# The FFN down projection by seven half-size products in four chunks of the contraction

## The chip, the cores and the metric

The kernel runs on one core of a Trainium2 chip. The metric is the device time of one execution in microseconds (us); lower is better.

## The reference

One decoder layer on 512 tokens with a model width of 2048. Only the last part matters here:

```python
x = x + gt_a * y                                   # called x1 below
h = rms_norm(x, g_ffn[l]) * (1.0 + sc_f) + sh_f    # h2 below
x = x + gt_f * conv_ffn(h, w_up[l], w_conv[l], b_conv[l], w_down[l])

def conv_ffn(h, w_up, w_conv, b_conv, w_down):
    u = h @ w_up                                   # 2048 -> 2 * 5632
    ...                                            # causal convolution, width 3, per channel
    gate, val = jnp.split(conv, 2, axis=-1)
    return (jax.nn.silu(gate) * val) @ w_down      # 5632 -> 2048
```

The product silu(gate) * val is called f. All data are float32. The gate gt_f is a vector over the 2048 output channels.

## The kernel before, in words

**Precision.** Every large matrix product is made of three TensorE products of float32r operands: each operand is split into a high half (a ScalarE copy into float32r) and a low half (a VectorE subtraction), and high x high, high x low and low x high are added up in PSUM. `split` (L112) does this for activations and, in `seven`, for weights; `wtile` (L95) loads and splits weights elsewhere.

**Buffers.** `get` and `put` hand out 81 slots of 128 x 512 floats from a first-in, first-out list. There are five raw weight buffers (`rawq`) and three pairs of split weight buffers (`hi_b`, `lo_b`). PSUM has eight banks of 128 x 512. SyncE (SP) issues the weight loads, GpSimd (POOL) issues the loads and stores of scratch tensors in DRAM. Each engine, and each issuing queue, goes through its instructions in order; the program's scheduler sets that order when the kernel is built, so it need not be the order of the code.

**The seven products.** `seven` (L912) multiplies a two-by-two block matrix of weights by a two-by-two block matrix of activations with seven block products in place of eight. For an output pair of two 128-channel tiles, the activations (split into halves of the contraction and halves of the 512 tokens) and four sums of them are prepared once: r11, r21, r22, t1 to t4. The weight blocks come per pair from DRAM (four loads), and VectorE makes four combinations of them. Each of the seven products is 8 contraction tiles x 3 matmuls of 256 columns, and one evacuation (`e1` to `e7`) of 128 x 256 takes it, or a sum in PSUM, out. Steps are prepared two ahead of their matmuls. The last gate columns (`w_gs`) and 40 of the 44 column pairs of the up projection (`w_ups`) are computed in this way.

**The end of the layer.** `ev_o` (L1238) makes x1 with tokens on the partitions and stores it to `x1_d` by 16 POOL transfers. `x1_T` (L1256) transposes it, and h2 is computed from it in place (L1292 to L1294). `up_group(0)` computes the first four f tiles in the ordinary way, `seven` the other 40; `ffn_out` applies the convolution and the gate and stores each f tile (channels on partitions) to `f_d` on POOL. Then the 44 tiles are loaded back into slots (L1377), four rows of the gate gt_f are loaded (`gate_row`), and the down projection runs twice over the 44 contraction tiles, once for each half of the output channels. Each step there loads 128 x 1024 weights, splits them, splits the f tile, and issues 8 banks x 3 matmuls of 512 columns, with tokens on the output partitions. Per bank the end is one multiplication with the gate row (L1406), one addition of x1 (L1407), and the store to the output (L1408).

**Gate columns.** `ada_stream` and `flush_cols` compute the modulation vectors during the mixer. Blocks named in `gtr_d` are written to DRAM as rows; the others go to columns of `mod` by two VectorE operations.

Of the kernel before, what the change touches and what calls it, by code (L numbers as in the profile page):

```python
# [31 lines left out]
def trunk_layer_kernel(  # L32
# [3 lines left out]
    g_mkv_lat, w_mkv_up, g_qm, g_km, w_pa, w_pb, w_o, w_up, w_ups, w_conv, b_conv, w_down,  # L36
# [13 lines left out]
    PEU=((2, 5, 8, 11, 14),) * 2 + ((),) * 6,  # L50
):
# [698 lines left out]
    gtr_d = {cb: dram.tile([P, T], F32, name=f"gtr{cb}") for cb in (8, 9, 10, 11, 20, 21, 22, 23)}  # L750
# [161 lines left out]
    def seven(src, n_pairs, rs, pairs_of_banks, fin, tick=None, near_end=None):  # L912
        r11, r21, r22, t1, t2, t3, t4 = rs

        def load(j, blk):
            t = rawq.popleft()
            SP.dma_start(t[:, :WN], src[j, blk])
            return t

        def hilo(t):  # L920
            i = cnt["wt"] % NH
            cnt["wt"] += 1
            hi, lo = hi_b[i][:, :WN], lo_b[i][:, :WN]
            split(hi, lo, t[:, :WN])
            return hi, lo

        def comb(o, a, b, op):
            V.tensor_tensor(o[:, :WN], a[:, :WN], b[:, :WN], op)  # L928

        def pair_steps(j):  # L930
            bx, by = pairs_of_banks[j % len(pairs_of_banks)]
            X, Y, Z = bx[:, :HT], by[:, :HT], by[:, HT:]
            L, E = {}, {}

            def p1():
                L[11] = load(j, 0)
                L[21] = load(j, 1)
                return hilo(L[11])

            def p7():  # L940
# [4 lines left out]
                L[22] = load(j, 3)  # L945
                return r

            def p6():
# [3 lines left out]
                L[12] = load(j, 2)  # L952
# [22 lines left out]
            def e1():  # L975
                E["s"] = get()
                A.activation(E["s"][:, :HT], X, AF.Copy)

            def e7():
                A.activation(E["s"][:, HT:], Y, AF.Copy)  # L980

            def e6():
                E["s6"] = get()
                A.activation(E["s6"][:, :HT], X, AF.Copy)

            def e2():
                E["u1"] = get()
                V.tensor_tensor(E["u1"][:, :HT], Z, E["s"][:, :HT], ALU.add)  # L988

            def e5():  # L990
                E["u2"] = get()
                V.tensor_tensor(E["u2"][:, HT:], X, E["s"][:, HT:], ALU.add)
                put(E["s"])

            def e4():
                V.tensor_tensor(E["u2"][:, :HT], Y, E["s6"][:, :HT], ALU.add)
# [9 lines left out]
        steps = [st for j in range(n_pairs) for st in pair_steps(j)]  # L1006
# [451 lines left out]
```

## Time and profile before

| what | value |
|---|---|
| median of 3 runs (lowest, highest) | 2702.99 us (2700.71, 2704.31) |
| the profiled execution's own time | 2702.67 us |
| its span, first to last instruction | 2700.9 us |
| TensorE, VectorE, ScalarE, GpSimd busy | 98%, 72%, 43%, 9% of the span |
| mean granted TensorE clock | 0.993 |
| DRAM traffic | 390.56 MB read, 44.04 MB written |

Durations in the profile come from one execution. PE is TensorE, PEld its weight loads, DVE VectorE, ACT ScalarE, POOL GpSimd, SP SyncE. A row of the groups reads: line, engine, operation, output<-inputs, shapes, count, then busy us and mean ns of one, then the engine's idle time just before these instructions and what ended it. In a row of the stretches, each engine's busy us in the stretch stands with its instruction count. In the waits a row reads: who waited, for whom, us in total, times, longest.

### The profile page before, as it was taken

What the parts mean: (1) busy time and instruction counts of PE and PEld (TensorE: products, weight loads), DVE (VectorE), ACT (ScalarE), POOL (GpSimd) and SP (SyncE); (2) the same over time, 40 slices, a digit from 0 to 9 for tenths busy, and PEclk for the clock granted to TensorE, in tenths of its full rate; (3) what the DMA queues carried; (4) which work ended last, traced back from release to release, by engine and by line L of the source; (5) the groups of instructions that cost most, each with busy time, mean ns of one, the idle gap of its engine ahead of it and who ended that gap; (6) DMA issues with size and microseconds to landing.
All of it is one profiled execution on the core that took longest, in us unless ns stands there. A gap on an engine that the chain in (4) does not pass through costs nothing.

```text
span 2700.9 us, 40414 instructions
## 1 busy us (share of the span) xinstructions
PE 2648.9 (98%) x15616; PEld 2298.6 (85%) x15616; DVE 1942.6 (72%) x3059; ACT 1154.9 (43%) x1711; POOL 237.1 (9%) x459
## 2 busy tenths in 40 slices
PE   6999999998999999999999999999999999999999
PEld 5777687778997767788789999999999998888887
DVE  7977976688878667983778888888888873325323
ACT  4333434334444555322545555555555553223221
POOL 1001011110022223110000000000000040000000
PEclk8999899999999999999999999999999999999999
DMA  9943136664585478973223333333333383233232
GB/s 340 343 158 98 33 112 207 202 214 159 182 273 165 147 257 277 334 275 133 91 95 121 117 126 118 118 122 114 125 122 118 122 308 118 97 121 126 97 116 75
DMA packets 198389, 437.26 MB, mean 162 GB/s; under 512 B 20106, under 2 KB 61476, under 8 KB 198196
## 3 DMA queue, kind: packets, MB, share of 16 engines
q1 hardware_dynamic: 166516, 348.60, 38.2%
q0 software_dynamic: 31648, 86.08, 9.5%
q8 instruction: 122, 2.00, 0.3%
q14 instruction: 71, 0.58, 0.1%
q10 hardware_dynamic: 32, 0.01, 0.0%
HBM read 390.56 MB, written 44.04 MB: 161 GB/s over the span
## 4 chain that ended last, share of the span: by engine, by line
PE 79%; issue 13%; DMA 4%; DVE 3%; POOL 1%; ACT 0%; SPq 0%; POOLq 0%; DVEq 0%; ACTq 0%
PE bank L117 15%; PE bank L118 14%; PE bank L119 14%; PE bank L1020 10%; PE bank L1021 10%; PE bank L1022 10%; DMA slot<-in_w_ada 2%; PE bank L1156 1%; DMA gate<-slot 1%; PE bank L683 1%; DVE slot L547 0%; DMA slot<-in_x 0%; DMA raw<-in_w_ada 0%; PE bank L1157 0%; PE bank L1154 0%
## 5 line engine op out<-in xcount | busy, mean ns | idle before, releaser
L1020 PE MATMUL bank<-slot,whi 128*128 128x256 f32 x2688 | 754.8, 282 | 9.8 <-DVE slot L988 4.6
L1021 PE MATMUL bank<-slot,whi 128*128 128x256 f32 x2688 | 754.6, 281 | 0.2 <-DVE slot L114 0.2
L1022 PE MATMUL bank<-slot,wlo 128*128 128x256 f32 x2688 | 749.1, 281 | 1.6 <-DVE wlo L114 1.6
L105 ACT ACTIVATE whi<-raw 128x1024 fp32r<-128x1024 f32 (+4 forms) x270 | 280.8, 1041 | 727.1 <-PE bank L119 525.2
L118 PE MATMUL bank<-wlo,slot 128*128 128x512 f32 (+2 forms) x1472 | 574.6, 391 | 0.9 <-DVE wlo L106 0.9
L117 PE MATMUL bank<-whi,slot 128*128 128x512 f32 (+2 forms) x1472 | 566.5, 392 | 6.5 <-ACT slot L384 4.9
L119 PE MATMUL bank<-whi,slot 128*128 128x512 f32 (+2 forms) x1472 | 569.7, 390 | 0.0
L113 ACT ACTIVATE whi<-raw 128x1024 fp32r<-128x1024 f32 x336 | 356.6, 1061 | 442.5 <-PE bank L1021 339.5
L106 DVE TENSOR_TENSOR wlo<-raw,whi 128x1024 fp32r<-128x1024 f32 (+4 forms) x270 | 323.4, 1198 | 276.9 <-ACT whi L105 274.9
L1020 PEld LDWEIGHTS bank<-slot,whi 128*128 128x128 f32 x2688 | 507.8, 189 | 12.6 <-DVE slot L988 5.4
L1021 PEld LDWEIGHTS bank<-slot,whi 128*128 128x128 f32 x2688 | 506.5, 188 | 0.6 <-DVE slot L114 0.5
L1022 PEld LDWEIGHTS bank<-slot,wlo 128*128 128x128 f32 x2688 | 504.0, 189 | 1.9 <-DVE wlo L114 1.8
L114 DVE TENSOR_TENSOR wlo<-raw,whi 128x1024 fp32r<-128x1024 f32 x336 | 409.7, 1220 | 84.2 <-ACT whi L113 83.5
L117 PEld LDWEIGHTS bank<-whi,slot 128*128 128x128 f32 x1472 | 278.2, 189 | 69.1 <-ACT slot L384 5.0
L118 PEld LDWEIGHTS bank<-wlo,slot 128*128 128x128 f32 x1472 | 278.4, 189 | 61.8 <-DVE wlo L106 1.4
L119 PEld LDWEIGHTS bank<-whi,slot 128*128 128x128 f32 x1472 | 276.8, 188 | 60.4 <-issue 0.5
L118 PE MATMUL bank<-slot,whi 128*128 128x512 f32 (+1 forms) x656 | 262.8, 401 | 1.3 <-DVE slot L686 1.3
L117 PE MATMUL bank<-slot,whi 128*128 128x512 f32 (+1 forms) x656 | 259.2, 403 | 1.7 <-ACT slot L1293 1.0
L928 DVE TENSOR_TENSOR raw<-raw,raw 128x1024 f32<-128x1024 f32 x192 | 234.6, 1222 | 31.9 <-DMA raw<-in_w_ups 24.5
L119 PE MATMUL bank<-slot,wlo 128*128 128x512 f32 (+1 forms) x656 | 256.8, 401 | 0.5 <-DVE wlo L106 0.5
L114 DVE TENSOR_TENSOR slot<-slot,slot 128x512 fp32r<-128x512 f32 x152 | 102.4, 687 | 181.7 <-PE bank L118 175.2
L722 DVE SCALAR_TENSOR_TENSOR slot<-slot,c_act,slot 128x512 f32<-128x512 f32 x203 | 150.0, 747 | 32.6 <-DMA slot<-in_w_ada 30.9
(288 smaller groups left out, 2518.8 us busy)
## 6 DMA issues: line engine op xcount, KB each, us to landing
slot<-in_w_ada SPq DMA_DIRECT2D x344, 256.0 KB, 5.6
raw<-in_w_ups SPq DMA_DIRECT2D x160, 512.0 KB, 3.2
raw<-in_w_down SPq DMA_DIRECT2D x88, 512.0 KB, 3.6
raw<-in_w_in SPq DMA_DIRECT2D x50, 512.0 KB, 3.4
raw<-in_w_gs SPq DMA_DIRECT2D x32, 512.0 KB, 3.3
raw<-in_w_o SPq DMA_DIRECT2D x32, 512.0 KB, 6.2
f<-slot POOLq DMA_DIRECT2D x44, 256.0 KB, 2.4
slot<-f POOLq DMA_DIRECT2D x44, 256.0 KB, 7.0
```

Source lines behind the costliest of these rows:

```text
L105: A.activation(hi, raw[:, :w], AF.Copy)
L106: V.tensor_tensor(lo, raw[:, :w], r32(hi), ALU.subtract)
L113: A.activation(dst_hi, src, AF.Copy)
L114: V.tensor_tensor(dst_lo, src, r32(dst_hi), ALU.subtract)
L117: PE.matmul(o, lh, rh, start=first, stop=False)
L118: PE.matmul(o, lh, rl, start=False, stop=False)
L119: PE.matmul(o, ll, rh, start=False, stop=last)
L722: V.scalar_tensor_tensor(acc, ts[i], c_act[:, k:k + 1], acc, op0=ALU.mult, op1=ALU.add)
L928: V.tensor_tensor(o[:, :WN], a[:, :WN], b[:, :WN], op)
L1020: PE.matmul(o, wh[:, ks], rh, start=first and k == 0, stop=False, skip_group_check=True)
L1021: PE.matmul(o, wh[:, ks], rl, start=False, stop=False, skip_group_check=True)
L1022: PE.matmul(o, wl[:, ks], rh, start=False, stop=last, skip_group_check=True)
```

## The change

The down projection is moved into `seven`. The 44 f tiles are taken in 22 couples (an even and an odd tile: the two halves of the contraction), and the couples are cut into four chunks of 6, 6, 5 and 5 (`DH`). In each chunk the 2048 output channels are done as eight pairs, with channels on the output partitions and tokens along the columns; a product has 6 or 5 contraction tiles, and weight blocks are 768 or 640 columns wide.

- `f_out` stores no f tile any more. It writes quarters of it, or adds them by accumulating DMAs, into seven DRAM tensors per couple: the operands r11, r21, r22 and the sums t1 to t4. Negated copies come from ScalarE.
- `ahead` loads these operand sets on SP and splits them, from the last five up pairs on for chunk 0, and from the middle of each chunk for the next one, as slots allow.
- The results of chunks 0 to 2, times the gate (now a column, a per-partition factor of the evacuation), are added to x1 in DRAM by accumulating DMAs. In chunk 3 the accumulated x1 is loaded and added during the evacuation, which is then VectorE's in all seven products, and the result goes to the output.
- x1 is stored transposed, from `x1_T` in place of `ev_o`. The gate blocks 20 to 23 become columns of `mod`. The output is written as channels x tokens and turned on the host, which is outside the device time; the weights of the down projection are laid out in blocks beforehand.

```diff
-    gtr_d = {cb: dram.tile([P, T], F32, name=f"gtr{cb}") for cb in (8, 9, 10, 11, 20, 21, 22, 23)}
+    gtr_d = {cb: dram.tile([P, T], F32, name=f"gtr{cb}") for cb in (8, 9, 10, 11)}
...
+    def seven(work, pairs_of_banks, hook=None):
+        def pair_steps(n, p):
+            bx, by = pairs_of_banks[n % len(pairs_of_banks)]
             X, Y, Z = bx[:, :HT], by[:, :HT], by[:, HT:]
             L, E = {}, {}
+            W = p.K * P
+            g1, g2 = p.scale or (None, None)
...
+            def copy(o, b, g, x):
+                if x is not None:
+                    V.scalar_tensor_tensor(o, b, g, x, op0=ALU.mult, op1=ALU.add)
+                elif g is not None:
+                    A.activation(o, b, AF.Copy, scale=g)
+                else:
+                    A.activation(o, b, AF.Copy)
+            def plus(o, b, g, x):
+                if g is not None:
+                    V.scalar_tensor_tensor(o, b, g, x, op0=ALU.mult, op1=ALU.add)
+                else:
+                    V.tensor_tensor(o, b, x, ALU.add)
...
-                A.activation(E["s"][:, :HT], X, AF.Copy)
+                copy(E["s"][:, :HT], X, g1, E["x10"])
...
-                V.tensor_tensor(E["u2"][:, HT:], X, E["s"][:, HT:], ALU.add)
+                plus(E["u2"][:, HT:], X, g2, E["s"][:, HT:])
...
-                A.activation(E["u1"][:, HT:], X, AF.Copy)
-                fin(j, E["u1"], E["u2"])
+                copy(E["u1"][:, HT:], X, g1, E["x11"])
+                if p.plus:
+                    put(*E["x"])
+                p.fin(E["u1"], E["u2"])
...
-            G.dma_start(x1_d[db][tb], xs[tb])
...
             A.activation(t, bk[m], AF.Copy)
+            G.dma_start(x1_d[db * 4 + m], t)
             x1T.append(t)
...
-    f_d = [dram.tile([P, T], F32, name=f"f{j}") for j in range(NF_)]
+    KINDS = ("r11", "t3", "t2", "r21", "t1", "t4", "r22")
+    f_d = {n: [dram.tile([P, HT], F32, name=f"f{n}_{i}") for i in range(NF_ // 2)] for n in KINDS}
+    def f_out(j, t):
+        i = j // 2
+        q1, q2 = t[:, :HT], t[:, HT:]
+        neg = get()
+        n1, n2 = neg[:, :HT], neg[:, HT:]
+        def add(n, v):
+            G.dma_start(f_d[n][i], v, accum_op=ALU.add)
+        if j % 2 == 0:
+            A.activation(neg, t, AF.Copy, scale=-1.0)
+            G.dma_start(f_d["t1"][i], q2)
+            G.dma_start(f_d["t4"][i], q2)
+            G.dma_start(f_d["t2"][i], q1)
+            G.dma_start(f_d["t3"][i], q2)
+            G.dma_start(f_d["r11"][i], q1)
+            add("t1", n1)
+            add("t4", n1)
+            add("t2", n2)
+        else:
+            A.activation(n2, q2, AF.Copy, scale=-1.0)
+            G.dma_start(f_d["r21"][i], q1)
+            G.dma_start(f_d["r22"][i], q2)
+            add("t4", q1)
+            add("t2", q2)
+            add("t3", n2)
+            add("t4", n2)
+        put(t, neg)
...
-    seven(w_ups, NF_ - 4, operands(h2, tsum), [(bank[2 * i], bank[2 * i + 1]) for i in range(4)], ffn_out)
-    for t in h2 + [x for ts in tsum for x in ts]:
-        put(*t)
-    fr = []
...
-            G.dma_start(xt, x1_d[db][tb])
-            V.tensor_tensor(o, bank[i], gf[db], ALU.mult)
-            V.tensor_tensor(o, o, xt, ALU.add)
-            SP.dma_start(out[tb * P:(tb + 1) * P, db * 512:(db + 1) * 512], o)
...
+    def load_set():
+        c, n = todo.popleft()
+        ts = []
+        for i in range(DH[c]):
+            if i % 2 == 0:
+                ts.append(get())
+            SP.dma_start(ts[-1][:, (i % 2) * HT:(i % 2 + 1) * HT], f_d[n][base[c] + i])
+        coming.append((c, n, ts))
+    def split_set():
+        c, n, ts = coming.popleft()
+        for i, t in enumerate(ts):
+            hi, lo = getr(), getr()
+            w = min(T, (DH[c] - 2 * i) * HT)
+            split(hi[:, :w], lo[:, :w], t[:, :w])
+            put(t)
+            held_by[c][n] += [hi, lo]
+            ops[c][n] += [(hi[:, o:o + HT], lo[:, o:o + HT]) for o in range(0, w, HT)]
+    def need(c):
+        return (DH[c] + 1) // 2
+    def ahead(left):
+        c = todo[0][0] if todo else coming[0][0] if coming else None
+        if c is None or left > 35 or left > 8 and left % 2:
+            return
+        if coming and len(free) >= 2 * need(coming[0][0]) + SPARE:
+            split_set()
+        if todo and todo[0][0] <= c and len(coming) < 2 and len(free) >= need(todo[0][0]) + SPARE:
+            load_set()
+    SPARE = 8
+    def up_hook(q, n):
+        last = q - (n - 7)
+        if last == 0:
+            for t in h2[:KH]:
+                put(*t)
+        elif last in (1, 2, 4, 5):
+            for t in tsum[{1: 2, 2: 1, 4: 0, 5: 3}[last]]:
+                put(*t)
+        elif last == 6:
+            for t in h2[KH:]:
+                put(*t)
+        ahead(n - q)
+    all_banks = [(bank[2 * i], bank[2 * i + 1]) for i in range(4)]
+    rs = operands(h2, tsum)
+    work = [Pair(rs, lambda blk, i=i: w_ups[i, blk], ffn_out(i)) for i in range(NF_ - 4)]
+    n_up = len(work) * 7
+    def down_pair(c, j):
+        def fin(u1, u2):
+            for i, u in enumerate((u1, u2)):
+                n = 2 * j + i
+                if c < len(DH) - 1:
+                    G.dma_start(x1_d[n], u, accum_op=ALU.add)
+                else:
+                    SP.dma_start(out[n * P:(n + 1) * P, :], u)
+            put(u1, u2)
+        def plus():
+            ts = [get(), get()]
+            for i in range(2):
+                G.dma_start(ts[i], x1_d[2 * j + i])
+            return ts
+        o = ops[c]
+        return Pair(tuple(o[n] for n in ("r11", "r21", "r22", "t1", "t2", "t3", "t4")),
+                    lambda blk: w_downs[c][j, blk], fin, K=DH[c],
+                    scale=(mod[:, 80 + 2 * j:81 + 2 * j], mod[:, 81 + 2 * j:82 + 2 * j]),
+                    plus=plus if c == len(DH) - 1 else None)
+    work += [down_pair(c, j) for c in range(len(DH)) for j in range(KD // 2)]
+    def hook(q, n):
+        if q < n_up:
+            up_hook(q, n_up)
+            return
+        c, r = divmod(q - n_up, 56)
+        if r >= 49:
+            put(*held_by[c][KINDS[r - 49]])
+        ahead(0 if (coming or todo or [(0,)])[0][0] == c else 56 - r)
+    seven(work, all_banks, hook)
```

More of the change, by code (lines that the diff above doesn't have):

```diff
@@ L910, in sum_tiles, with __init__ @@
             put(raw[n])
[L912 to L931, printed above, removed]
+    class Pair:
+        def __init__(self, rs, load, fin, K=KH, scale=None, plus=None):
+            self.rs, self.load, self.fin, self.K, self.scale, self.plus = rs, load, fin, K, scale, plus
```

153 lines of the change are left out of this document (82 added, 71 removed).

## The prediction

> **What bounds the kernel now.** I read the page first, then the busy time by stretches, the groups by line and shape, the waits, and the timelines of the seams.
>
> ```profile
> span 2700.9 us, 40414 instructions
> PE 2648.9 (98%) x15616; PEld 2298.6 (85%) x15616; DVE 1942.6 (72%) x3059; ACT 1154.9 (43%) x1711; POOL 237.1 (9%) x459
> DVE  7977976688878667983778888888888873325323
> PEclk8999899999999999999999999999999999999999
> ```
> TensorE carries the span at an undisturbed clock; VectorE is high in the up projection (slices 21 to 32) and low in the down projection (the last eight). The stretches say it in numbers (busy us of PE, PEld, DVE, ACT, POOL, then clock, DMA share, GB/s):
>
> ```profile
> 1440.00:1640.00 200.00, 200.00 (x1691) 200.00 (x1690) 174.54 (x191) 108.59 (x141) 5.40 (x10) 1.00 0.34 120
> 2160.00:2200.00 40.00, 40.00 (x340) 40.00 (x339) 35.48 (x42) 25.29 (x36) 14.92 (x28) 1.00 0.71 251
> 2300.00:2400.00 100.00, 100.00 (x432) 80.77 (x431) 29.67 (x29) 24.40 (x30) 3.76 (x7) 1.00 0.33 113
> ```
> So both stages are bound by how many columns TensorE must stream. The change takes columns away from the down stage and gives VectorE work there: the question is whether VectorE still keeps up. The seams of the stage, from the PE timeline and the chain that ended last:
>
> ```profile
> 2202.20 0.28 PE L1022 MATMUL bank<-slot,wlo 128*128 128x256 f32 x1
> 2204.08 0.50 PE L117 MATMUL bank<-whi,slot 128*128 128x512 f32 x1 [1.60 <-ACT slot L113]
> 2694.20 0.47 issue
> 2696.58 0.69 DVE slot L1407
> ```
> Up ends at 2202.5, down runs 2204.1 to 2694.2 (490.1 us), and two VectorE operations and the last store end the span at 2700.9.
>
> **TensorE's part.** Before, down issues 2 halves x 44 tiles x 8 banks x 3 = 2112 matmuls of 512 columns: 490.1 / 2112 = 232.06 ns each. After, it issues 8 pairs x 7 products x 22 tile positions (6+6+5+5) x 3 = 3696 of 256 columns. Their price stands in the up stage, which runs the same seven products:
>
> ```profile
> L977 ACT ACTIVATE slot<-bank x40: 362/367/371, 1409.8 to 2186.3; 128x256 f32<-128x256 f32 x40
> ```
> This is the first evacuation of each pair: 39 pairs in 776.5 us, 19.91 us each, 168 matmuls of 118.54 ns. So 3696 x 118.54 = 438.1 us, **52.0 us less**. The two prices (232.06 and 118.54) give 5.0 ns fixed per matmul; the 1584 more matmuls cost 8 us of it, inside the term.
>
> The Trainium skill, "TensorE: Matmul & The Clock Gate", section "Back-to-back issue gap", speaks against this: sustained spacing 81 ns at 128 columns and 131 at 512, so halving the columns saves far less than half. A straight line between its figures puts 256 columns at 0.75 of 512, and the term would be an estimated 640 us. The trace disagrees: 118.54 against 232.06 is 0.51.
>
> **VectorE's part.** A pair splits seven weight blocks and makes four combinations, each K x 128 columns wide, now 768 or 640 instead of 1024, and the products are taken out with the gate as a factor.
>
> ```profile
> L114 DVE TENSOR_TENSOR wlo<-raw,whi 128x1024 fp32r<-128x1024 f32 x336 | 409.7, 1220 | 84.2 <-ACT whi L113 83.5
> L114 DVE TENSOR_TENSOR slot<-slot,slot 128x512 fp32r<-128x512 f32 x152 | 102.4, 687 | 181.7 <-PE bank L118 175.2 <-ACT slot L113 3.3 <-DMA raw<-in_w_down 3.1
> L988 DVE TENSOR_TENSOR slot<-bank,slot 128x256 f32<-128x256 f32 x48 | 20.0, 417 | 0.4 <-PE bank L1022 0.4
> L1303 DVE SCALAR_TENSOR_TENSOR slot<-slot,wcv,slot 128x511 f32<-128x511 f32 x80 | 59.6, 745 | 0.0
> L1364 DVE TENSOR_TENSOR slot<-slot,slot 128x512 f32<-128x512 f32 x40 | 27.4, 684 | 0.0
> L1323 DVE SCALAR_TENSOR_TENSOR slot<-slot,mod,slot x8: 470/473/476, 1334.7 to 1363.6; 128x256 f32<-128x256 f32 x8
> ```
> On the line through 687 and 1220 ns, 768 columns take 0.95 us and 640 take 0.82. An up pair sums to 11 x 1.22 + 3 x 0.417 + 4 x 0.745 + 0.684 = 18.3 us, while the first stretch shows 174.54 of 200, 17.4 a pair: neighbours overlap, a factor of 0.95. Down, by the same counting, with the next chunk's operand sets (21 splits of 0.687; for a five-tile chunk 14 and 7 of half size) spread over eight pairs, against 18 or 15 matmuls a product:
> - chunk 0: 11 x 0.95 + 3 x 0.47 + 1.8 = 13.7, times 0.95 = 13.0 of 14.9 us (87%); chunk 1: 12.7 (85%)
> - chunk 2: 9.0 + 1.4 + 1.6 = 12.0, so 11.3 of 12.45 us (91%)
> - chunk 3, where all seven evacuations are VectorE's (x1 is added there): 9.0 + 7 x 0.47 = 12.3, so 11.6 (94%).
>
> The up stage holds TensorE full at 87%. What fills its remaining 13%, from the waits between 1440 and 2160:
>
> ```profile
> ACT whi L113 <- PE bank L1021: 254.0, 212, 1.8
> DVE wlo L114 <- ACT whi L113: 68.8, 95, 1.6
> DVE raw L928 <- DMA raw<-in_w_ups: 19.0, 37, 2.2
> ```
> VectorE waits 1.9 us a pair for the high half and 0.5 for weights (36.2 pairs), but the high half itself mostly waits for TensorE to free its buffer: backpressure, which shrinks once TensorE has to wait. Chunks 2 and 3 lie between nothing and all 2.4 us kept: 13.7 and 14.0 against 12.45, 1.3 and 1.6 us a pair, 23 us together. I take a quarter, **+6 us**, as the backpressure row is the nearest.
>
> **The seams.** Entry into chunk 0: its seven sets can get their slots only when the first half of h2 is given back after the first product of the last up pair, so 21 splits fall on that pair. ScalarE's prices:
>
> ```profile
> L113 ACT ACTIVATE whi<-raw 128x1024 fp32r<-128x1024 f32 x336 | 356.6, 1061 | 442.5 <-PE bank L1021 339.5 <-issue 78.9 <-PE bank L118 12.0
> L113 ACT ACTIVATE slot<-slot 128x512 fp32r<-128x512 f32 x152 | 91.6, 621 | 47.7 <-DVE slot L722 14.9 <-DVE slot L1040 7.0 <-DVE slot L1407 5.6
> ```
> VectorE needs (18.3 + 21 x 0.687 + 11.9) x 0.95 = 42.4 us for the last up pair and the first down pair, TensorE 34.8. Of the 7.5 over, two prepared products (2 x 2.1) cover 4.3. ScalarE has 10.8 + 21 x 0.62 + 7.4 = 31 us in the same 34.8, so the two wait on each other. The gap, 1.6 now, is between 0 and 12; I take **6**. Inside the stage each change of chunk bursts the last three sets at the start of the last pair, 3 x 2.06 us with about the same cover: 0 to 3 each, **3 together**. End: one 256-column VectorE operation instead of two of 512, then the same store (the last started after 2696.58 + 0.69 and took until 2700.9): 6.7 becomes **4.8** (4 to 6).
>
> **Moved to POOL.** f goes out as seven sums. Per two tiles POOL issues 7 writes and 7 adds instead of 2 writes.
>
> ```profile
> L1365 POOL DMA_DIRECT2D f<-slot x40 | 21.6, 541 | 715.5 <-DVE slot L1364 714.6 <-DVE slot L992 0.9
> L773 POOL DMA_DIRECT2D slot<-in_b_ada x8: 848/888/923, 1036.9 to 2225.5; - x8
>   DMA slot<-gtr: 8.5, 4
> DMA to landing us min/median/max: 6.4/7.8/9.8
> ```
> The existing add costs 0.89 us to issue and lands after 7.8. Seven writes and seven adds are 10 us, and t4's last add waits behind its earlier one: about 17 of the 39.8 us that two tiles take, on an engine busy 5.4 in 200. Traffic rises by 14 transfers of 128 KB and 7 re-reads less the two old 256 KB writes in 39.8 us, some 55 GB/s on 120, which the 2160 stretch (251) bears with PE full. ScalarE's negations are 0.62 us on 10.8 of 19.9. All zero, covered by those idle shares. If the adds fell behind, the slots they read would not come free (rivals).
>
> The Trainium skill, "DMA: Bandwidth & Descriptors", section "Rules for kernel authors", demands such a wait between an accumulate and any other access to the same bytes; the trace agrees, with the add's wait for the load above (8.5 us, four times).
>
> The set loads (154 on SP) queue behind weight loads that wait for raw buffers; the oldest two sets are fetched several pairs ahead, the others one or two products ahead, which the gap's upper bound holds. The x1 stores move behind the transposes, ahead of the reciprocal root on POOL:
>
> ```profile
> 1312.07 2.13 ACT L1261 ACTIVATE slot<-bank 128x512 f32<-128x512 f32 x4
> 1311.77 1.03 POOL L221 TENSOR_TENSOR rstd<-rsm,mhalf 128x4 f32<-128x4 f32 x1 [3.16 <-DVE rsm L220]
> 1314.05 0.69 DVE L242 COPY slot<-bank 128x512 f32<-128x512 f32 x1 [2.37 <-PE bank L240]
> ```
> In strict order the root starts after the twelfth copy (1314.2) and its issue, 3 us late, and h2 behind it; if the queue is ordered by readiness, nothing. **+1** (0 to 4). The last gate columns' extra VectorE work (two short operations) fits into the 2.37 us it waits there. The gate rows' reloads and the 44 reloads of f go away, hidden now and worth nothing.
>
> **Sum.** 2202.5 + 1 + 6 + 438.1 + 3 + 6 + 4.8 = 2661.4 span. The profiled execution took 2702.67 for its span of 2700.9, so +1.8: **2663**, 39.5 below it; the median of the runs shown, 2702.99, stands 0.3 above it, which is noise.
>
> **Rivals.**
> - *All hidden.* Every seam and wait at its lower bound: 2202.5 + 438.1 + 4 + 1.8 = 2646; up to 2655 counts here. For: TensorE never waits in the up stage. Against: 94% in chunk 3. Chance 0.20.
> - *VectorE paces the stage.* Its 2.4 us of waits stay in full: chunks 0 and 1 lose 0.4 and 0.2 us a pair, 2 and 3 the 1.3 and 1.6: 28 us in place of 9, 2682; with the wider seams 2692. Chance 0.18.
> - *Slower: every split waits for its high half.* Place: the in-order VectorE queue of all 32 pairs, where a low half stands behind its high half with nothing in front. 7 x 0.84 or 7 x 0.73 exposed plus 0.5 for weights give pairs of 19.4, 19.1, 16.9, 17.2 us, 143 us over TensorE's time: near 2797. It decides from about 3.1 us of waits a pair, where the 1.5 us that VectorE has free on average and the 49 us of gain are used up. Against: 2.4 now, with longer operations. Chance 0.08.
> - *POOL's adds run in series.* If each of the 14 transfers of two tiles waited for a landing, adds alone would take 7 x 7.8 = 55 us of 39.8, and slots would pace the up stage: +300 us. It decides from 39.8. Against: six of the seven sums are independent tiles. Chance 0.03.
> - *Weight loads pace the short products.* If the loads, which overlap now, ran one after the other, 3696 of 0.188 us would be 695 us in place of 438: 2920. Against: 118.54 ns spacing with the same loads. Chance 0.01. The page "TensorE: Matmul & The Clock Gate" of the Trainium skill leans this way.
>
> ```profile
> L1021 PEld LDWEIGHTS bank<-slot,whi 128*128 128x128 f32 x2688 | 506.5, 188 | 0.6 <-DVE slot L114 0.5
> ```
>
> The forecast itself (2655 to 2675) has 0.50. The range 2647 to 2692 leaves out little but the slow cases. A measurement here tells about 0.2% (5 us) from no change. Faster is 0.50 + 0.20 + 0.18 = 0.88 and slower 0.08 + 0.03 + 0.01 = 0.12; taking 0.01 from each for a cancelling mixture gives faster 0.87, same 0.02, slower 0.11.
>
> **What would show it.** Right: matmuls of 256 columns still 118 to 119 ns apart down to the end; VectorE at 85 to 95% there; PE gaps of some microseconds at the entry and in chunks 2 and 3. Wrong: spacing above 125 ns, a long list of PE waits for wlo or for evacuated banks, POOL busy without pause in the up stage, or pairs of the up stage longer than 19.9 us.

## The result and the profile after

| | before | after |
|---|---|---|
| median (lowest, highest) | 2702.8 us (2700.71, 2704.31) | 2750.99 us (2750.22, 2755.43) |
| profiled execution, span | 2702.67, 2700.9 us | 2751.13, 2749.4 us |

The changed kernel takes 1.0182 times the time of before, with a 95% interval of 1.0165 to 1.02: 48 us slower, where 39 us faster was forecast and the range ended at 2692. The page of the kernel after, in the lines that answer to those of before, and of its transfers the weight blocks of the up projection and the writes of f (KB each, median us to landing):

```profile
span 2749.4 us, 45335 instructions
PE 2633.1 (96%) x17200; PEld 2360.8 (86%) x17200; DVE 2154.1 (78%) x3427; ACT 1278.1 (46%) x1979; POOL 443.2 (16%) x715
DVE  7977967698888658863868888888888887777788
raw<-in_w_ups SPq DMA_DIRECT2D x160, 512.0 KB, 4.4
ft<-slot POOLq DMA_DIRECT2D x242, 128.0 KB, 4.6
```

TensorE is busy for 16 us less than before, not 52, and idle for 64 us more. The stretches say where (columns as in the prediction). First one in the up stage, then from the down stage the entry, pairs four to six of chunk 0, the change to chunk 1, middle pairs of chunk 1, the change to chunk 2, and chunk 3:

```profile
1440.00:2140.00 700.00, 682.95 (x5677) 676.07 (x5676) 584.65 (x644) 372.31 (x508) 168.41 (x235) 1.00 0.56 149
2220.00:2260.00 40.00, 29.58 (x214) 28.48 (x213) 35.37 (x52) 26.55 (x46) 5.49 (x9) 0.91 0.82 248
2300.00:2340.00 40.00, 37.91 (x320) 37.71 (x319) 30.66 (x38) 19.09 (x30) 5.11 (x6) 1.00 0.66 155
2380.00:2420.00 40.00, 32.80 (x244) 31.91 (x243) 27.95 (x38) 17.86 (x29) 3.41 (x4) 0.91 0.60 155
2420.00:2460.00 40.00, 39.44 (x332) 39.24 (x332) 29.46 (x37) 19.06 (x29) 5.11 (x6) 1.00 0.63 154
2500.00:2540.00 40.00, 32.59 (x231) 31.43 (x230) 29.37 (x45) 20.72 (x38) 3.43 (x4) 0.87 0.71 188
2660.00:2700.00 40.00, 39.81 (x338) 39.63 (x337) 36.60 (x59) 17.39 (x24) 0.54 (x1) 1.00 0.52 158
```

Read the count of matmuls, not only the busy time: 40 us hold 338 of them at full rate. Chunk 3, where VectorE is at 92%, is full; the entry and the changes, where VectorE is at 70 to 88%, hold 214 to 244. The up stage, untouched in its products, has 5677 matmuls in 700 us, where before fits 5908.

The same in pairs: the time from one pair's last evacuation to the next one's, from the timelines of ScalarE and VectorE, added up by chunk (us). The first row is what TensorE alone needs at 118.54 ns. "Last" is the last up pair, 20.2 us before. The other rows are the experiments below, each in one profiled execution; a lost record shifts a sum by about 1 us.

```
kernel      up pair   last   chunk 0   chunk 1   chunk 2   chunk 3     span
TensorE       19.92   19.9     119.5     119.5      99.6      99.6
after         20.74   30.4     140.5     133.4     123.0     100.5   2749.4
a_noadd       19.94   30.9     138.9     134.9     123.0      99.9   2721.9
a_plain       20.55   28.8     141.7     133.2     120.3     100.9   2742.3
d_dve         19.93   25.6     142.6     135.5     120.4     101.0   2715.6
d_pool        20.00   26.3     139.8     137.2     120.8     100.7   2725.0
b_reuse       20.67   27.7     124.1     119.2     110.4     101.2   2704.9
b_noload      20.58   24.9     142.6     136.2     114.6     101.8   2739.0
c_noxadd      20.79   30.1     129.3     127.0     106.3     100.3   2719.6
f_ring        20.65   31.0     133.2     127.4     113.1     100.0   2725.8
e_spread      19.99   28.0     128.5     129.7     111.2     102.1   2692.9
e_early       19.99   26.7     134.1     129.8     109.7     100.5   2698.9
g_pri         20.01   27.0     130.7     130.1     117.2      99.3   2700.6
g_poolq       19.94   20.9     134.5     124.7     111.5     100.1   2682.8
```

The after kernel's pairs of chunk 0 are 18.9, 18.7, 17.6, 16.3, 14.9, 14.9, 16.2 and 22.8 us: the middle ones are exactly TensorE's 14.94, and the loss stands at the entry and beside the change of chunk. Three questions follow: what slows the up stage by 31 us (38 x 0.82), what costs 59 us at the seams of the down stage (497.4 against 438.2), and whether a version without these causes wins.

### The profile page after: what moved, and what is told of

Same layout as the page of the kernel before. It is cut to its first block, busy times and chain, and to the rows that moved or that the text cites. A ratio compares the mean times of both kernels' runs of the same rounds, so it can differ in the third digit from the quotient of the medians.

```text
span 2749.4 us, 45335 instructions
## 1 busy us (share of the span) xinstructions
PE 2633.1 (96%) x17200; PEld 2360.8 (86%) x17200; DVE 2154.1 (78%) x3427; ACT 1278.1 (46%) x1979; POOL 443.2 (16%) x715
## 4 chain that ended last, share of the span: by engine, by line
PE 56%; issue 19%; DMA 13%; DVE 9%; POOL 2%; ACT 2%; SPq 0%; DVEq 0%; POOLq 0%; ACTq 0%
PE bank L118 9%; PE bank L119 9%; PE bank L120 9%; PE bank L1050 8%; PE bank L1051 8%; PE bank L1052 8%; DMA raw<-in_w_ups 6%; DVE wlo L115 3%; DMA slot<-in_w_ada 2%; DVE raw L941 2%; POOL x L1506 1%; DMA raw<-in_w_ada 1%; ACT whi L114 1%; DMA gate<-slot 1%; PE bank L1194 1%
## 5 line engine op out<-in xcount | busy, mean ns | idle before, releaser
L1050 PE MATMUL bank<-slot,whi 128*128 128x256 f32 x3920 | 1116.0, 285 | 77.9 <-ACT slot L947 27.9
L1051 PE MATMUL bank<-slot,whi 128*128 128x256 f32 x3920 | 1108.1, 283 | 0.4 <-DVE slot L115 0.4
L1052 PE MATMUL bank<-slot,wlo 128*128 128x256 f32 x3920 | 1100.2, 283 | 2.0 <-DVE wlo L115 2.0
L1050 PEld LDWEIGHTS bank<-slot,whi 128*128 128x128 f32 x3920 | 746.7, 191 | 95.9 <-DVE slot L955 36.0
L114 ACT ACTIVATE whi<-raw 128x1024 fp32r<-128x1024 f32 (+2 forms) x560 | 531.8, 951 | 561.6 <-PE bank L1051 386.4
L1051 PEld LDWEIGHTS bank<-slot,whi 128*128 128x128 f32 x3920 | 745.1, 190 | 0.7 <-DVE slot L115 0.6
L1052 PEld LDWEIGHTS bank<-slot,wlo 128*128 128x128 f32 x3920 | 741.9, 190 | 2.8 <-DVE wlo L115 2.6
L115 DVE TENSOR_TENSOR wlo<-raw,whi 128x1024 fp32r<-128x1024 f32 (+2 forms) x560 | 606.8, 1086 | 80.4 <-ACT whi L114 78.0
L941 DVE TENSOR_TENSOR raw<-raw,raw 128x1024 f32<-128x1024 f32 (+2 forms) x320 | 348.5, 1089 | 143.9 <-DMA raw<-in_w_ups 109.6
L119 PE MATMUL bank<-wlo,slot 128*128 128x512 f32 (+2 forms) x768 | 297.6, 388 | 0.9 <-DVE wlo L107 0.9
L118 PE MATMUL bank<-whi,slot 128*128 128x512 f32 (+2 forms) x768 | 290.3, 391 | 4.4 <-ACT slot L385 3.9
L120 PE MATMUL bank<-whi,slot 128*128 128x512 f32 (+2 forms) x768 | 293.3, 386 | 0.0
L118 PEld LDWEIGHTS bank<-whi,slot 128*128 128x128 f32 x768 | 146.0, 190 | 35.8 <-ACT slot L385 4.0
L120 PEld LDWEIGHTS bank<-whi,slot 128*128 128x128 f32 x768 | 144.9, 189 | 29.2 <-issue 0.5
```

The lines of the kernel that those rows point to most:

```text
L114: A.activation(dst_hi, src, AF.Copy)
L115: V.tensor_tensor(dst_lo, src, r32(dst_hi), ALU.subtract)
L118: PE.matmul(o, lh, rh, start=first, stop=False)
L119: PE.matmul(o, lh, rl, start=False, stop=False)
L120: PE.matmul(o, ll, rh, start=False, stop=last)
L941: V.tensor_tensor(o[:, :W], a[:, :W], b[:, :W], op)
```

## Experiments on the up stage

**Half the transfers, and plain ones.** Theory: the seven adds per two tiles delay the weight blocks; rival: something else of the new up stage, such as ScalarE's negations or the slots held by `f_out`. `a_noadd` drops the adds, `a_plain` keeps their number but writes to spare tensors.

```diff
-            G.dma_start(f_d[n][i], v, accum_op=ALU.add)
+            return                                       # a_noadd
+            G.dma_start(spare_d[spare_n[0]], v)          # a_plain
+            spare_n[0] += 1
```

> Leaves out the seven accumulating writes of f per couple (the operands t1 to t4 are then incomplete); the seven plain writes stay. Theory (the adds take DMA time from the weight loads, VectorE gets its weight blocks late and TensorE its evacuated banks): up pairs go from 20.75 back to 19.9-20.0 us, the waits of VectorE for w_ups from 98 to about 25 us, time 2751 - 31 = 2720 (2713 to 2727). Rival (the number of POOL transfers or the negations on ScalarE): half of the transfers are left, so at most half comes back: 2735 or more.

> Each of the seven adds becomes a plain write of the same bytes into a spare DRAM tile (t1 to t4 incomplete). Same number of transfers and bytes out of SBUF, no reading back of the destination and no waiting for an earlier write. Theory (it is the accumulating kind): most comes back, up pairs at 20.2 or less, 2722 to 2730. Rival (any 128 KB transfer costs the weight loads as much): pairs stay at 20.6 or more, 2745 to 2751.

Measured: 2724.14 and 2744.03 us (before beside them 2700.98). The stretch 1440 to 2140 of before, of `a_noadd` and of `a_plain`:

```profile
1440.00:2140.00 700.00, 699.79 (x5908) 699.59 (x5907) 610.50 (x669) 377.73 (x492) 18.91 (x35) 1.00 0.34 120
```
```profile
1440.00:2140.00 700.00, 699.38 (x5901) 698.78 (x5900) 605.77 (x667) 391.94 (x527) 65.72 (x123) 1.00 0.43 132
```
```profile
1440.00:2140.00 700.00, 687.17 (x5718) 680.80 (x5718) 587.92 (x648) 375.26 (x512) 128.50 (x242) 1.00 0.47 150
```

With seven transfers per two tiles TensorE is full (5901 matmuls), with fourteen it isn't, whether they add or only write. So the number of transfers, or their traffic, costs most of the 31 us. The accumulating kind costs little of it: 20.55 us a pair in place of 20.74 is 7 us over the stage, but the four other kernels of the table that keep the adds (`b_reuse`, `b_noload`, `c_noxadd`, `f_ring`) have 20.58 to 20.79, so this difference is hardly larger than their spread. The path runs through VectorE. The waits of after between 1440 and 2140 (us in total, times, longest):

```profile
DVE raw L941 <- DMA raw<-in_w_ups: 91.3, 67, 2.8
POOL ft L1359 <- DMA ft<-slot: 69.0, 44, 4.0
PE bank L1050 <- DVE slot L955: 16.5, 26, 1.9
```

Before, the first of these was 18.8 us in the same window and the last 0.2; no split and no evacuation waits there for a slot that a write of f still reads. The weight blocks' own times to landing (min, median, max), in this window of before and of after:

```profile
DMA to landing us min/median/max: 3.0/3.2/5.0
```
```profile
DMA to landing us min/median/max: 3.4/4.4/6.7
```

They are issued from the same queue into the same five buffers and arrive 1.2 us later; VectorE combines them late, evacuates late, and TensorE waits for a bank. The median alone does not sort the kernels: it is 3.5 in `d_dve` (below), 3.6 in `a_noadd` and 3.8 in `d_pool`, which keep TensorE full, and 3.9 in `a_plain`, which doesn't. VectorE's waits for the blocks do: 41 to 44 us in the first three, 86 in `a_plain`. ScalarE's negations, which `a_noadd` keeps, cost nothing.

**The sums made on an engine.** `d_dve` holds the even tile until the odd one is there, makes t1 to t4 by four subtractions on VectorE and writes seven plain transfers, without negated copies; `d_pool` does the same on GpSimd. The theory was that VectorE has room for them; the rival, that it then paces the stage.

```diff
-            add("t1", n1) ... add("t4", n2)
+        V.tensor_tensor(t1, q2, q1, ALU.subtract)      # G. in d_pool
+        V.tensor_tensor(t2, p2, t1, ALU.subtract)
+        V.tensor_tensor(t3, q2, p2, ALU.subtract)
+        V.tensor_tensor(t4, p1, t2, ALU.subtract)
```

> The whole result again: f tiles are held for a couple, VectorE makes the four sums (four operations of 256 columns per couple, 4 x 0.418 us), and seven plain writes of 128 KB go out in place of fourteen transfers. Theory (the number of transfers beside the weight loads sets the up pairs): as with the adds left out, pairs of 19.9 to 20.1 us, 2751 - 27 = 2722 (2716 to 2728). Rival (VectorE, now 91% in that stage, takes the place of the transfers): pairs of 20.4 or more, 2738 or more.

> The same with the four sums on GpSimd. If the sums are hidden on either engine: 2722 as with VectorE's, up pairs 19.9 to 20.1. If GpSimd's operations hinder VectorE: rows of VectorE longer than 1.22 us for 1024 columns and pairs above 20.3.

Measured: 2717.38 and 2726.78 us (before beside them 2703.17). The stretch of `d_dve`:

```profile
1440.00:2140.00 700.00, 699.88 (x5909) 699.68 (x5908) 631.71 (x740) 376.69 (x491) 66.77 (x125) 1.00 0.44 133
```

VectorE goes from 87% to 90% and TensorE is full again. So the up stage's loss is undone, at 34 us less than after. GpSimd is a poor place for the same four subtractions. The first of them (min, median, max ns), and VectorE's splits in the same window of `d_pool` and then of `d_dve`:

```profile
L1363 POOL TENSOR_TENSOR slot<-slot x22: 737/1646/2470, 1415.1 to 2213.6; 128x256 f32<-128x256 f32 x22
```
```profile
L115 DVE TENSOR_TENSOR wlo<-raw,whi 128x1024 fp32r<-128x1024 f32 x245 | 321.4, 1312 | 19.4 <-ACT whi L114 19.1
```
```profile
L115 DVE TENSOR_TENSOR wlo<-raw,whi 128x1024 fp32r<-128x1024 f32 x247 | 301.1, 1219 | 22.5 <-ACT whi L114 22.1
```

VectorE's 256-column addition took 417 ns in the prediction's rows. GpSimd's operations also lengthen VectorE's splits, 1.31 us in place of 1.22, one of the two signs that the expectation named; the other, pairs above 20.3, did not come: the up pairs of `d_pool` are 20.0 us. Of its 9.4 us over `d_dve`, 7.0 lie in the later first up pair (1436.5 against 1429.6). That says little: `e_early` and `g_poolq`, which have `d_dve`'s code up to there, end this pair at 1435.0 and 1429.9.

## Experiments on the seams of the down stage

**Without the set work.** `b_reuse` lets chunks 1 to 3 use chunk 0's operand sets, so that nothing is loaded or split after the entry. `b_noload` splits every set of these chunks from one resident tile: splits, but no loads.

```diff
-    todo = deque((c, n) for c in range(len(DH)) for n in KINDS)
+    todo = deque((0, n) for n in KINDS)                          # b_reuse
+            split(hi[:, :w], lo[:, :w], res[:, :w])              # b_noload
```

> Chunks 1 to 3 use chunk 0's operand sets: no set loads and no splits after the entry (results of chunks 1 to 3 are of the wrong f). Theory (the down stage loses its time to the fetching of the next sets at chunk changes): the losses of the last pairs of chunks 0 to 2 and the first of 1 to 3, 9 + 14 + 23 = 46 us, vanish: 2705 (2698 to 2715); the entry's stays. Rival (x1's accumulating DMAs, the evacuation with a factor on ScalarE, or short products pace it): 2735 or more.

> From chunk 1 on the splits read one resident tile in place of the loaded sets: the same splits at the same places and the same slots taken, but no set loads on SP (chunks 1 to 3 compute with wrong f). Theory (the loads do it: SP's queue stands at slots that x1's adds still read, the weight loads wait behind, ScalarE's splits wait for landings and the evacuations behind them): 2710 to 2720. Rival (the burst of splits on ScalarE and VectorE): 2740 or more.

Measured: 2706.71 and 2741.33 us. The set work costs 44 us, nearly all of it in chunks 0 to 2 (table). The loads alone cost at most 10, and of these only 2 in the down stage (495.2 against 497.4): the theory of `b_noload` (2710 to 2720) is missed, its rival (2740 or more) holds. `b_reuse` keeps a loss of 11 us in chunk 2, without any set work. There VectorE waits 14.8 us for weight blocks in 110, in chunk 1 only 1.4 in the same time; the accumulating adds into x1 come in both, but chunk 2's pairs are a sixth shorter, and the blocks land after 3.8 us (median) in place of 3.2:

```profile
DVE raw L941 <- DMA raw<-in_w_down: 14.8, 12, 2.6
```

Twelve of the sixteen loads of x1 for chunk 3 are issued beside these pairs of `b_reuse` too (2507 to 2584), which after issues only from 2630 on; whether these or the adds delay the blocks was not separated.

**Without the adds into x1.** The waits of after in the down stage (2150 to 2750) name the set work, and something behind it:

```profile
PE bank L1050 <- ACT slot L947: 27.9, 18, 5.1
DVE raw L941 <- DMA raw<-in_w_down: 24.6, 36, 3.7
ACT slot L114 <- DMA slot<-fr: 15.0, 8, 3.2
ACT slot L114 <- DMA x<-slot: 14.1, 6, 3.3
PE bank L1050 <- ACT whi L114: 11.8, 6, 4.4
```

The fourth line is not a wait for data. ScalarE's split of a set waits for `x<-slot`, an accumulating add that still reads the slot which the split wants to write: `down_pair` gives u1 and u2 back as soon as the add is issued. Where the set loads are left out, the splits meet the adds themselves, which fits the little that `b_noload` won. Its waits from 2225 to 2700 (after: 14.1 and 3.6 us):

```profile
ACT slot L114 <- DMA x<-slot: 26.7, 11, 3.9
DVE slot L115 <- DMA x<-slot: 11.2, 6, 2.6
```

On SP the third line below says the same of the set loads (queue waits of after, 2225 to 2700):

```profile
SPq L930 <- DVE wlo L115: 189.9, 75, 5.9
SPq L930 <- DVE raw L941: 84.6, 23, 8.8
SPq L1454 <- DMA x<-slot: 35.7, 11, 5.9
```

These queues go in order, so the weight loads behind the set load stand too. `c_noxadd` leaves the adds out.

```diff
-                    G.dma_start(x1_d[n], u, accum_op=ALU.add)
+                    pass
```

> The changed kernel without the accumulating DMAs into x1 (chunks 0 to 2 are evacuated and dropped; the output holds chunk 3's part alone). Theory (SP's set loads wait 36 us in all for slots that these adds still read; this is a part of what the loads cost): chunks 0 to 2 lose 5 to 12 us less, 2739 to 2746. Rival (the adds' traffic slows the weight loads of the down stage as f's do in the up stage): 20 us or more, 2730 or less.

Measured: 2721.51 us, 29 less than after (34.5 in the down stage). The 5 to 12 us that the theory of set work alone gave to the adds are missed. But this run takes away two things, the adds' traffic and their hold on the slots.

**Only the hold taken away.** `f_ring` keeps every add and gives the evacuated pairs of the down stage four slots of their own, used in turn, so that no set load or split meets a pending add.

```diff
+        ring_n[0] += 1
+        return ring[(ring_n[0] - 1) % 4]
...
-    SPARE = 8
+    SPARE = 6
...
-            put(u1, u2)
...
-                    plus=plus if c == len(DH) - 1 else None)
+                    plus=plus if c == len(DH) - 1 else None, u=ring_u)
```

> The changed kernel with one edit: the evacuated pairs of the down stage take turns in four slots of their own instead of going through the common first-in, first-out list (the reserve of the fetching is lowered from 8 to 6 slots so that sets are fetched at the same products). The adds to x1 stay, all of them. Leaving the adds out won 29 us. Theory (slots come back to the sets' loads and splits while an add still reads them, and the in-order queues of SP, ScalarE and VectorE stand at them): most of the 29 comes back with the adds in place, 2722 to 2732. Rival (the adds' DMA traffic itself): 2744 or more.

Measured: 2727.56 us (before beside it 2702.76), 23 less than after. On SP the wait for `x<-slot` is no longer among the larger ones; what a set load waits for now is VectorE:

```profile
SPq L930 <- DVE wlo L115: 206.7, 88, 5.9
SPq L930 <- DVE raw L941: 81.3, 26, 4.7
SPq L1463 <- DVE slot L953: 24.5, 15, 4.1
```

So of the 59 us at the seams some 23 come from slots that are reused under a pending add. The down stage of `c_noxadd` is another 11 us shorter than that of `f_ring` (462.9 against 473.7, one execution each), which the traffic of the adds may cost. How the chain goes on to TensorE shows in ScalarE's timeline at the change to chunk 1 (start, us, and in brackets the idle time and who ended it), and in TensorE's:

```profile
2372.43 0.63 ACT L114 ACTIVATE slot<-slot 128x512 fp32r<-128x512 f32 x1 [3.22 <-DMA slot<-fr]
2372.97 0.83 ACT L114 ACTIVATE whi<-raw 128x768 fp32r<-128x768 f32 x1
2373.70 0.46 ACT L947 ACTIVATE slot<-bank,mod 128x256 f32<-128x256 f32 x1
```
```profile
2374.21 0.39 PE L1050 MATMUL bank<-slot,whi 128*128 128x256 f32 x1 [2.55 <-ACT slot L947]
```

ScalarE stands 3.2 us before a split whose load is late; the evacuation two places behind it is late by as much, and TensorE stands 2.55 us for the bank. The longest wait of the entry (5.1 us for `L947`) looks the same: seven places ahead of the evacuation, ScalarE stood 4.3 us before a split whose load was late. But the ring leaves the entry as it was (31.0 us for the last up pair), and no run takes the entry's loss apart.

**Part of a gap is paid again.** In the down stage of after 155 matmuls start some 0.21 us behind the one before them in place of 0.1185, which adds 15 us. Of these, 116 stand in seven runs of 14 to 22, which add 11 us; the others are single ones, mostly the first behind a gap. The runs stand where the granted clock, the seventh number of a stretch, is at half. Two stretches at the change to chunk 1, and two in chunk 0:

```profile
2382.09:2385.50 3.41, 1.24 (x10) 1.03 (x9) 3.31 (x7) 2.13 (x4) 0.63 (x1) 1.00 0.91 271
2385.50:2388.91 3.41, 3.41 (x19) 3.41 (x18) 3.32 (x5) 0.00 (x1) 0.22 (x1) 0.50 0.91 252
2269.45:2272.86 3.41, 1.90 (x17) 1.69 (x15) 0.29 (x2) 1.68 (x3) 0.00 (x0) 1.00 0.89 174
2272.86:2276.27 3.41, 2.58 (x21) 2.58 (x22) 2.48 (x4) 2.14 (x5) 0.00 (x0) 1.00 0.24 57
```

In the first, TensorE stands 2.17 us (up to 2385.03), and in the second only 16 matmuls start in place of 28.8 (the row also counts those that reach into it). The other two hold a gap that is longer, 2.34 us (up to 2273.69), and the clock stays. The trace shows the difference. Each stretch at half clock lasts 3.41 us or twice that, and their starts lie whole multiples of 3.413 us apart (2375.26, 2385.50 and 2395.74 are three steps apart each). Of the windows of this grid from 1400 us on, the nine at full clock that are followed by one at half clock held TensorE busy for at most 46%, all the others for 49% or more. A border of the grid cuts the gap of 2.34 us in two, and its windows are 56 and 76% busy. So it is not the length of the gap that decides, but whether TensorE is busy for less than about half of such a window; in six of the other traces the limit lies between 45 and 51%.

## Experiments towards a version that beats both

**Sums on VectorE, ring, spread sets.** `e_spread` joins `d_dve` and the ring of `f_ring`, and hands out loads and splits one tile at a time, ten of a chunk's 21 up to the eighth product ahead of the chunk, the others one per product. Chunk 0's sets, at the entry, come tile by tile too, at a pace of their own.

```diff
+    def wanted(c, tau):          # tau: products until the chunk begins
+        ...
+            l = (tau + 52) // 2
+            p = (tau + 46) * 10 // 38 if tau < -7 else 10 + tau + 8
```

> VectorE's sums as in the other run, and the operand sets fetched and split tile by tile: next chunk's 21 tiles are loaded one per two products, 10 of them split evenly over the first six pairs and the rest one per product around the change; the evacuated pairs of chunks 0 to 2 keep four slots of their own, so no load waits for a slot that an add to x1 still reads. Theory (burst of splits, with late loads, at chunk changes): the 44 us over the steady pairs at the three changes fall to 12 or less: 2722 - 32 = 2690 (2678 to 2700). Rival (any splits in the stage make ScalarE's evacuations late, since ScalarE goes in order): the losses spread over all pairs and 2712 or more.

Measured: 2694.86 us in one execution, the first version below before (2703.17 beside it). Against `f_ring` the down stage gained only 2 us (471.5 against 473.7 in the table's sums): the spreading itself did little.

**Fourteen tiles early.** `e_early` splits 14 of the 21 early and loads four tiles ahead of the split.

```diff
-            l = (tau + 52) // 2
-            p = (tau + 46) * 10 // 38 if tau < -7 else 10 + tau + 8
+            p = (tau + 50) * 14 // 42 if tau < -7 else 14 + (tau + 8) * 7 // 11
+            l = p + 4 if tau >= -54 else 0
```

> As the run with the sets spread tile by tile, but 14 of a chunk's 21 tiles are split before the change instead of 10 (loads run only four tiles ahead), and the other seven over eleven products around it. Theory (what is left at the changes, 24 us over the steady pairs, is still the density of splits there): 2684 to 2690, about 0.5% below the kernel before the change. Rival (the remaining losses are the weight loads at a change of chunk or the adds' traffic): 2693 or more.

Measured: 2693.13 us (2690.53 to 2700.64; the profiled execution is the longest of them), 0.9964 of before with an interval of 0.995 to 0.9978. The theory's 2684 to 2690 is missed. Splits still wait for the loads:

```profile
ACT slot L1457 <- DMA slot<-fr: 13.2, 9, 2.6
ACT slot L1457 <- DMA slot<-ft: 8.0, 4, 2.7
```

**The loads brought forward.** They are issued four tiles ahead in the code, but SP's queue takes them where the scheduler puts them. `g_pri` raises their priority, `g_poolq` issues them from GpSimd instead.

```diff
+        with tc.high_priority(offset=1000):              # g_pri
...
-            SP.dma_start(t[:, h * HT:(h + 1) * HT], f_d[n][base[c] + 2 * i + h])
+            G.dma_start(t[:, h * HT:(h + 1) * HT], f_d[n][base[c] + 2 * i + h])     # g_poolq
```

> As the run with 14 tiles split early, with one edit: the loads of the set tiles are ordered ahead of other work on SP's queue. In that run ScalarE's splits still waited 21 us for set loads to land, which SP issued in a bunch just before each change. Theory (late landings hold ScalarE, and the evacuations behind it): 2676 to 2686. Rival (the density of the splits): within 3 us of 2693.

> As the run with 14 tiles split early, with one edit: GpSimd's queue issues the loads of the set tiles, so that SP's holds weights and output only. Theory (set loads and weight loads hold each other up in one queue): 2676 to 2688. Rival: GpSimd's queue stands at the adds to x1, which wait for evacuations, and the loads come later still: 2695 or more.

Measured: `g_pri` 2701.88 us, 0.9999 of before (0.999 to 1.0008), worse than `e_early` and outside what either theory gave it; why was not settled. `g_poolq` 2689.72 us (2684.57 to 2690.97; the profiled execution is the shortest of them), 0.9957 of before (0.994 to 0.9973), just over the 2676 to 2688 expected. Its waits from 2190 to 2700 no longer have a split that waits for a set load among the larger ones, and TensorE's largest is 11.1 us, the longest 1.9, where after had 27.9 and 5.1:

```profile
POOL slot L1448 <- DVE slot L1458: 81.4, 11, 12.5
DVE raw L941 <- DMA raw<-in_w_down: 39.9, 38, 3.4
PE bank L1050 <- DVE slot L953: 11.1, 10, 1.9
```

It is the fastest version run, 0.4% below before. Against `e_early` its interval overlaps, so the move of the queue by itself isn't shown to pay.

## Why the prediction was wrong, step by step

The forecast span was 2661.4, the measured one 2749.4. The 88 us between them, by the prediction's own terms:

| term | forecast | measured | difference |
|---|---|---|---|
| x1 transposed before its store | +1 | +3.1 at the end of the first up pair | +2 |
| writes and adds of f in the up stage | 0 | 38 pairs x 0.82 | +31 |
| last up pair | part of the entry's 6 | 30.4 for 20.2 | +10 |
| matmuls of the down stage | 438.1 | 438.2 at full rate | 0 |
| rest of the entry, changes of chunk, pace of chunks 2 and 3 | 6 + 3 + 6 | 59 | +44 |
| end | 4.8 | 3.6 | -1 |

(The remaining 1 to 2 us is where up's end is put, 2202.5 or the evacuation at 2203.9. The first row is one execution: the end of the first up pair, 1426.9 before and 1430.0 after, comes at 1432.8 to 1433.4 in `f_ring`, `c_noxadd`, `b_noload` and `b_reuse`, whose code up to there does the same work.)

**The first failing step is "Moved to POOL ... All zero, covered by those idle shares".** The cost on GpSimd was right: the adds did not run in series, and their waits for an earlier transfer (69.0 us in 700) cost no more than the 7 us by which plain writes were faster. What the step left out is the receiver of the contention. It took the 2160 stretch, 251 GB/s with PE full, as proof that the traffic is borne; after, 149 GB/s were enough to stop TensorE, at a DMA share of 0.56 (0.47 in `a_plain`, 0.44 in `d_dve`, which loses nothing). That stretch lasted 40 us, and its issues show the opposite of what the step read from it (number, KB each, median us to landing):

```profile
slot<-f POOLq DMA_DIRECT2D x26, 256.0 KB, 7.3
raw<-in_w_down SPq DMA_DIRECT2D x5, 512.0 KB, 8.8
raw<-in_w_ups SPq DMA_DIRECT2D x4, 512.0 KB, 3.3
```

The last block of the up stage is issued at 2177, ahead of most of the reloads of f. The first blocks of the down stage, issued beside them from 2183 on, land after 8.8 us, where the page of before has 3.6; PE was full because nothing waited for these blocks yet. And no row of before has fourteen transfers of 128 KB per two pairs, so the cost should have been bounded from both sides and not set to nothing. The Trainium skill, "DMA: Bandwidth & Descriptors", section "Issuing engines are not separate DMA queues", states that DMAs started by the scalar, sync or gpsimd engine run on the same 16 DMA engines and interleave. The trace agrees (4.4 against 3.2 us to landing). Two signs that the prediction had named for being wrong came with it: up pairs longer than 19.9 us, and TensorE's waits for evacuated banks.

**The second is the seams: "0 to 3 each, 3 together" and the entry's "6", with 12 as its upper end.** The pairs give 22 us at the entry (10 in the last up pair and 12 in the first four down pairs), then 18, 21 and 9 at the three changes. The work was counted rightly, 21 splits a chunk, but as if engine time were all. Three things were missed: a slot is not free when it is given back but when the last add has read it (23 us, `f_ring`); a set load or split that waits holds the in-order queue with weight loads and evacuations behind it; and a window of 3.41 us in which TensorE is busy for less than about half is followed by one at half clock (11 us of the down stage, inside the 59). The 23 us lie at the changes; what the entry's 22 us consist of was not taken apart.

**Right.** Spacing: 338 matmuls in 40 us are one per 118 ns, against a forecast of 118 to 119. The figures of the Trainium skill, "TensorE: Matmul & The Clock Gate", section "Back-to-back issue gap" (81 ns at 128 columns, 131 at 512), by which half the columns would take an estimated 0.75 of the time, do not fit this kernel: the traces have 118 against 232 ns, 0.51. VectorE's prices and its margin:

```profile
L115 DVE TENSOR_TENSOR wlo<-raw,whi 128x768 fp32r<-128x768 f32 x112 | 106.2, 955 | 33.0 <-ACT whi L114 31.3
L115 DVE TENSOR_TENSOR wlo<-raw,whi 128x640 fp32r<-128x640 f32 x112 | 91.4, 819 | 13.8 <-ACT whi L114 13.3
L953 DVE SCALAR_TENSOR_TENSOR slot<-bank,mod,slot 128x256 f32<-128x256 f32 x96 | 45.9, 479 | 12.1 <-PE bank L1052 12.1
```

0.95, 0.82 and 0.47 us were forecast. Steady pairs take 14.9 us, and the last seven of chunk 3 a mean of 12.3, TensorE's time: there the 6 us for VectorE's pace did not come, and the rival in which it paces the whole stage falls. (The 11 us of chunk 2 in `b_reuse`, 1.35 a pair, are of the size that this rival gave to that chunk, but that run brings transfers into the chunk that after doesn't have there.) The rival in which every split waits for its high half falls as well: these waits are 44.6 us and those for weights 24.6 over 32 pairs, 2.2 a pair together, where 3.1 were needed. The other rivals did not occur either. None named the weight stream slowed by GpSimd's transfers, which needed no queue to fall behind.

Open: how the 33 to 39 us that remain in the down stage of the versions with the ring divide between the entry, the dense splits and late weight blocks; why a higher priority lengthened `g_pri`; and how much of `a_plain`'s loss is the number of transfers and how much their bytes, since both double together.

## What to carry to other kernels

A stretch that keeps TensorE full beside some traffic for 40 us does not show that a stage of 780 us bears it: look up in that stretch how late the loads landed and whether anybody was waiting for them yet, then ask how much lateness the buffers ahead absorb. When a buffer goes back to a shared list with a transfer still reading it, look up who gets it next and what is queued behind that instruction; a few private buffers were worth 23 us here. A gap at a seam costs more than its length where it leaves TensorE busy for less than about half of a clock window.

## What the runs showed of the hardware

- Matmuls of 256 columns start 118.5 ns apart at a granted clock of 1.00 and some 213 ns apart at 0.50. The clock is at half for 3.41 us or twice that, on a fixed grid of 3.413 us, and goes there behind a window in which TensorE was busy for less than about half (at most 46% in after, where 49% and more had no effect).
- Fourteen transfers of 128 KB per two pairs (39.8 us at full rate) bring a stream of 512 KB loads from 3.2 to 3.9 us to landing as plain writes and to 4.4 with half of them accumulating, and TensorE loses 3 to 4% of the stage; seven bring it to 3.5 to 3.8 and TensorE stays full. Beside 26 reloads of 256 KB in 40 us a 512 KB load took 8.8.
- Two-input operations of 256 columns on GpSimd (median 1.65 us) lengthen VectorE's 1024-column splits beside them from 1.22 to 1.31 us.
- An accumulating add costs 857 ns (median) of GpSimd to issue and lands after 4.8, at most 8.6 us:

```profile
L1506 POOL DMA_DIRECT2D x<-slot x48: 840/857/1195, 2266.3 to 2647.4; - x48
DMA to landing us min/median/max: 3.9/4.8/8.6
```
